# Output projection of a hybrid encoder layer: two blocks by seven products of quarters in place of eight

## The chip, the cores and the metric

The kernel runs on one core of one Trainium2 chip. The metric is the device time of one execution in microseconds (us); lower is better. A core has a matrix engine (TensorE, PE in the profile, with its weight loads as PEld), a vector engine (VectorE, DVE), a scalar engine (ScalarE, ACT), a general engine (GpSimd, POOL) and a queue that issues the transfers here (SyncE, SP). Each works through its own list of instructions in order and waits on semaphores for the others.

## The reference

One layer over 4096 tokens of width 1024, all float32:

```python
h = rmsnorm(x, pre_norm_g)
q, k, v, g_a, u_p, g_p = split(h @ w_in)            # 512, 128, 128, 512, 512, 512 columns
a = banded_attention(q, k, v, rel_bias, attn_sink) * silu(g_a)   # |i-j| <= 128, 8 query heads, 2 of k and v
p = multiscale_pool(u_p, pool_w, pool_scale) * silu(g_p)         # centred means over 2, 4, 8, 16 tokens
mixed = concatenate([a, p], -1) @ w_out             # (4096, 1024) @ (1024, 1024)
x = x + rmsnorm(mixed, post_norm_g)
```

The change touches the line of `mixed`, and what prepares its operands.

## The kernel before

Every float32 operand of a matmul is carried as a pair of float16 (high part and rest), so each product takes three matmuls: high·high, high·rest of the weights, rest·high.

**First phase** (from 0 to 541 us): eight tiles m of 512 tokens. For each, x is normalised, split into a pair (`x_split`, one `xp` tile per block of 128 tokens) and transposed by DMA into `xt`; then TensorE makes twelve projections of it: u, gp and ga, four each of 128 columns. ACT and DVE evacuate them; the pooled rows go to DRAM as float16 pairs (`yp_scr`), the gates as `ga_scr`, the x pairs as `x_scr`. The weights are scaled and split between, in a list `todo`; `prep_out`, which prepares w_out (8 tiles `wop`, 16 stores to `w_scr`), runs during tile 6. The `wop` tiles share the two buffers "xp" with the split x.

**Second phase** (from 541 us): pairs u of 128-token blocks, from u = 15 down, block 2u+1 ahead of 2u. TensorE's order is written by hand here (`manual_schedule`); the other engines' and SP's lists are ordered by the framework's scheduler. Per pair: `proj_kv`, two halves of `proj_q`; per block two halves of `softmax` (s on TensorE, the maximum on DVE, the exponential on ACT, the normalised pair `pn` on ACT and DVE, and a DMA transpose by SP to `pt`); `attend` (the attention output o on TensorE, gated on DVE, split on ACT and POOL into `ya`); `output` (96 matmuls of 512 columns per pair: for each block and each half of the columns 8 row blocks × 3, reading the pair `yb` of pooled rows from DRAM and `ya`), then squares on ACT, the norm's power on POOL, and the sum with x on DVE. `output` runs one block behind `attend`. The accumulators of kv, q and output rotate over three PSUM banks; there are two `pn` and four `pt` buffers.

Of the kernel before, what the change touches and what calls it, by code (L numbers as in the profile page):

```python
# [17 lines left out]
P = 128  # L18
# [8 lines left out]
PT_BUFS = 4  # L27
# [12 lines left out]
YLAG = 1  # L40

UT = 2 * P
NU = S // UT

# [8 lines left out]
GP_EVAC = 2.0**-29  # L53
GA_EVAC = 2.0**-43
# [4 lines left out]
def hybrid_layer(ctx: ExitStack, tc, io, out):  # L59
# [6 lines left out]
    gemm = ctx.enter_context(tc.tile_pool(name="gemm", bufs=3, space=PSUM))  # L66
# [27 lines left out]
    yp_scr = dram.tile([NB, P, 4, 2, P], F16, name="yp_scr")  # L94
    ga_scr = dram.tile([NB, P, 4, P], F32, name="ga_scr")
    w_scr = dram.tile([2, P, KT, D], F16, name="w_scr")
# [16 lines left out]
    def project(name, wh, wl, x, with_last=False):  # L113

        acc = gemm.tile([P, T], F32, name=name, tag="acc")
        a3 = acc.rearrange("p (b t) -> p b t", b=BPM)
        n = 0
        for k in range(KT):
            for w, kk in ((wh, k), (wl, k), (wh, KT + k)):
                mm = nc.tensor.matmul(  # L120
                    a3, w[:, k, :], x[:, :, kk, :], start=(n == 0), stop=(n == 3 * KT - 1)
                )
                n += 1
        return (acc, mm) if with_last else acc
# [5 lines left out]
    with ExitStack() as actx:  # L130
# [202 lines left out]
        def prep_out():  # L333
# [13 lines left out]
                out=rowsc[:, 0:4], in0=rowsc[:, 0:4], scalar1=2.0**23, scalar2=None, op0=ALU.mult  # L347
            )
            nc.vector.scalar_tensor_tensor(
                out=rowsc[:, 4:8], in0=rowsc[:, 4:8], scalar=2.0**24, in1=psc,  # L350
# [26 lines left out]
            for k in range(KT):  # L377
                w = pa.tile([P, D], F32, name=f"wo_b{k}", tag="wraw", bufs=4)
                nc.sync.dma_start(w, io["w_out"][k])
                s = rowsc[:, k : k + 1]  # L380
                wp = pa.tile([P, 2, D], F16, name=f"wop{k}", tag="xp", bufs=2)
                nc.scalar.activation(wp[:, 0], w, AF.Copy, scale=s)
                nc.vector.scalar_tensor_tensor(
                    out=wp[:, 1], in0=w, scalar=s, in1=wp[:, 0], op0=ALU.mult, op1=ALU.subtract
                )
                for i in range(2):
                    nc.sync.dma_start(w_scr[i, :, k, :], wp[:, i])
# [12 lines left out]
        def pool_tile(m, j, u, sg):  # L400

            yp = pa.tile([P, BPM, 2, P], F16, name=f"yp{m}_{j}", tag="yp")
            w = 2 << j
            cur, n = u, T + 16
            for lv in range(j + 1):
                n -= 1 << lv
                nxt = pa.tile([P, T + 16], F32, name=f"ws{m}_{j}_{lv}", tag="ws")
                nc.vector.tensor_tensor(
                    out=nxt[:, :n], in0=cur[:, :n], in1=cur[:, (1 << lv) : (1 << lv) + n],
                    op=ALU.add,  # L410
                )
# [16 lines left out]
            nc.gpsimd.tensor_tensor(out=t, in0=t, in1=sg, op=ALU.mult)  # L428
            t3 = t.rearrange("p (b t) -> p b t", b=BPM)
# [4 lines left out]
            nc.sync.dma_start(  # L434
                yp_scr[m * BPM : (m + 1) * BPM, :, j].rearrange("b p c d -> p b c d"), yp
            )
# [28 lines left out]
        first = gemm.tile([P, T], F32, name="gp0_0", tag="acc")  # L465
# [89 lines left out]
    wo_h = pb1.tile([P, KT, D], F16, name="wo_h")  # L555
    wo_l = pb1.tile([P, KT, D], F16, name="wo_l")
# [31 lines left out]
    def proj_kv(u):  # L588
        x = x_half(u)
        acc = gemm.tile([P, 2, UT], F32, name=f"kv{u}", tag="acc")  # L590
# [17 lines left out]
    def proj_q(u, half):  # L608

        x = x_half(u)  # L610
        if half == 0:
            q_t[u] = pb.tile([P, 2, 4, UT], F16, name=f"q{u}", tag="q")
        acc = gemm.tile([P, 2, UT], F32, name=f"q{u}_{half}", tag="acc")
        for jj in range(2):
            project_t(acc[:, jj], B_Q + 2 * half + jj, x)
        js = slice(2 * half, 2 * half + 2)
        split(q_t[u][:, 0, js], q_t[u][:, 1, js], acc)

    pt, y_t = {}, {}
# [4 lines left out]
    def softmax(b, half):  # L624
# [21 lines left out]
        for jj in range(2):  # L646
# [3 lines left out]
            for n, (qi, ki) in enumerate(((0, 0), (1, 0), (0, 1))):  # L650
                for c0, c1, kc in segs:
                    for gg in range(2):
                        a = slice(64 * gg, 64 * gg + 64)
                        nc.tensor.matmul(  # L654
                            s_ps[:, gg, c0:c1], q_t[u][a, qi, j0 + jj, tl : tl + P],
                            k_all[a, ki, kc : kc + c1 - c0], start=(n == 0 and c0 == 0),
                            stop=(n == 2 and c1 == nk), skip_group_check=True,
                        )
# [16 lines left out]
        pn = pb.tile([P, 2 * 4 * 3 * P], F16, name=f"pn{b}_{g}", tag="pn")  # L675
# [11 lines left out]
        nc.sync.dma_start(t4, pn[:, : 8 * nk], transpose=True)  # L687
        pt[b, half] = t4.rearrange("p (v g j k) q -> p v g j k q", v=2, g=2, j=2)

    def attend(b):  # L690
# [19 lines left out]
        y = pb.tile([P, 4, 2, P], F16, name=f"ya{b}", tag="ya", bufs=YLAG + 3)  # L710
        t = pb.tile([P, 4, P], F32, name=f"at{b}", tag="at")
        nc.vector.tensor_tensor(out=t, in0=o_ps, in1=ga, op=ALU.mult)  # L712
        nc.scalar.copy(y[:, :, 0], t)  # L713
        nc.gpsimd.tensor_tensor(out=y[:, :, 1], in0=t, in1=y[:, :, 0], op=ALU.subtract)  # L714
        y_t[b] = y

    def output(b):
        ya = y_t.pop(b)
        yp = pb.tile([P, 4, 2, P], F16, name=f"yb{b}", tag="yb")
        nc.sync.dma_start(yp, yp_scr[b])  # L720
        xr = pb.tile([P, D], F32, name=f"xr{b}", tag="xr")
        nc.sync.dma_start(xr, io["x"][b * P : (b + 1) * P, :])
        ss = pb.tile([P, 2], F32, name=f"ss{b}", tag="ss")
        mo = pb.tile([P, D], F32, name=f"mo{b}", tag="mo")
        for c in range(2):
            cs = slice(c * 512, (c + 1) * 512)
            acc = gemm.tile([P, 512], F32, name=f"mx{b}_{c}", tag="acc")
            n = 0
            for k in [4, 5, 6, 7, 0, 1, 2, 3]:
                y = yp[:, k - 4] if k >= 4 else ya[:, k]  # L730
                for yi, w in ((0, wo_h), (0, wo_l), (1, wo_h)):
                    nc.tensor.matmul(  # L732
                        acc, y[:, yi, :], w[:, k, cs], start=(n == 0), stop=(n == 3 * KT - 1)
                    )
                    n += 1
            junk = pb.tile([P, 512], BF16, name=f"jkb{b}_{c}", tag="junk", bufs=1)
            nc.scalar.activation(  # L737
                junk, acc, AF.Square, scale=2.0**-5, accum_out=ss[:, c : c + 1]
            )
            nc.vector.tensor_tensor(out=mo[:, cs], in0=acc, in1=gpost[:, cs], op=ALU.mult)  # L740
        ms = pb.tile([P, 1], F32, name=f"msb{b}", tag="ms")
        nc.vector.tensor_scalar(  # L742
            out=ms, in0=ss[:, 0:1], scalar1=ss[:, 1:2], scalar2=epss, op0=ALU.add, op1=ALU.add
# [3 lines left out]
        for cs in (slice(0, 512), slice(512, D)) if b == 0 else (slice(0, D),):  # L747
# [6 lines left out]

    with tc.manual_schedule(engines={mybir.EngineType.PE}):
# [3 lines left out]
        nc.sync.dma_start(wo_h, w_scr[0])  # L759
        nc.sync.dma_start(wo_l, w_scr[1])  # L760
# [3 lines left out]
        waiting = []  # L764
        for b in reversed(range(NB)):
            u = b // 2
            softmax(b, 0)
            if b == NB - 1:
                proj_q(u, 1)
                load_x(u - 2)  # L770
            if b % 2:
                if u > 0:
                    proj_kv(u - 1)
            else:
                if u > 0:
                    proj_q(u - 1, 0)
            if b == 0:
                output(waiting.pop(0))
            late = b in (NB - 2, NB // 2 - 1)
            if b + 1 < NB and not late:  # L780
                attend(b + 1)
                waiting.append(b + 1)
            softmax(b, 1)
            if b % 2 == 0 and u > 0:
                proj_q(u - 1, 1)
                load_x(u - 3)
            if late:
                attend(b + 1)
                waiting.append(b + 1)

            if len(waiting) > YLAG and b != NB // 2:
                output(waiting.pop(0))
        while waiting:
            output(waiting.pop(0))
        attend(0)
        output(0)
# [72 lines left out]
```

## Time and profile before

| | |
|---|---|
| median of 3 runs | 1282.33 us (1282.01 to 1283.87) |
| profiled execution | 1281.24 us, span 1279.4 us |
| first phase / second phase | 0 to 541 / 541 to 1279.4 us |
| matmuls of `mx` (output projection) | 1536, in four groups by operand of about 163, 163, 97 and 97 us busy |
| matmuls of all kinds | 8824 |

The profile shows one execution: busy time and count of each engine, groups of instructions by line with mean durations in ns, the chain of work that ended last, and the waits between engines. Matmuls overlap in the records, so what one costs is the distance from one to the next and not its duration. In a row such as `pt<-pn` the tile written stands left, the one read right. A row's bracket gives the engine's idle time ahead of it, and who ended it.

### The profile page before, as it was taken

What the parts mean: (1) busy time and instruction counts of PE and PEld (TensorE: products, weight loads), DVE (VectorE), ACT (ScalarE), POOL (GpSimd) and SP (SyncE); (2) the same over time, 40 slices, a digit from 0 to 9 for tenths busy, and PEclk for the clock granted to TensorE, in tenths of its full rate; (3) what the DMA queues carried; (4) which work ended last, traced back from release to release, by engine and by line L of the source; (5) the groups of instructions that cost most, each with busy time, mean ns of one, the idle gap of its engine ahead of it and who ended that gap; (6) DMA issues with size and microseconds to landing.
All of it is one profiled execution on the core that took longest, in us unless ns stands there. A gap on an engine that the chain in (4) does not pass through costs nothing. (4 is left out here: it accounts for less than half of the span.)

```text
span 1279.4 us, 22210 instructions
## 1 busy us (share of the span) xinstructions
PE 1245.6 (97%) x8824; PEld 718.4 (56%) x8824; DVE 732.0 (57%) x1609; ACT 588.4 (46%) x1271; POOL 197.5 (15%) x247
## 2 busy tenths in 40 slices
PE   4999999999999999999999999999999999999997
PEld 3643444444444444476666667577657666665643
DVE  5577373819151546456656557567656666575562
ACT  6365242515121541156555546456645555464451
POOL 1023131414030313301000101001100101010011
PEclk9998999999999999999999999999999999999999
DMA  7669385818170671287685777767666757755572
GB/s 229 231 162 288 145 217 146 256 49 277 52 206 25 204 224 42 70 264 169 169 186 132 174 165 160 162 158 172 167 161 154 191 138 171 178 143 128 126 191 90
DMA packets 331576, 210.19 MB, mean 164 GB/s; under 512 B 266656, under 2 KB 301088, under 8 KB 328528
## 3 DMA queue, kind: packets, MB, share of 16 engines
q1 hardware_dynamic: 331472, 208.78, 62.3%
q8 instruction: 69, 1.13, 0.4%
q14 instruction: 35, 0.29, 0.1%
HBM read 90.24 MB, written 52.99 MB: 112 GB/s over the span
## 5 line engine op out<-in xcount | busy, mean ns | idle before, releaser
L120 PEld LDWEIGHTS <-wa_h 128*128 128x128 f16 x1520 | 149.0, 98 | 184.9 <-issue 7.9
L667 ACT ACTIVATE p<-p,nm 128x385 f32<-128x385 f32 (+1 forms) x256 | 152.9, 599 | 49.3 <-POOL rsb L746 43.0
L583 PE MATMUL q<-xt,wb_h 128*128 128x256 f16 x1024 | 173.2, 273 | 0.0
L681 DVE SCALAR_TENSOR_TENSOR pn<-p,rd,pn 128x384 f16<-128x384 f32 (+1 forms) x256 | 139.4, 607 | 44.5 <-ACT pn L678 44.4
L732 PE MATMUL mx<-wo_h,ya 128*128 128x512 f16 x512 | 162.7, 379 | 0.2 <-POOL ya L714 0.2
L732 PE MATMUL mx<-wo_h,yb 128*128 128x512 f16 x512 | 162.9, 379 | 0.0
L120 PE MATMUL u<-xt,wa_h 128*128 128x512 f16 x512 | 155.7, 382 | 4.3 <-DVE xp L169 4.3
L662 DVE CUSTOM_DVE_ANT_0 p<-s,bias,nsink 128x384 f32<-128x384 f32 (+1 forms) x256 | 155.9, 664 | 0.5 <-PE s L654 0.5
L120 PE MATMUL ga<-xt,wa_h 128*128 128x512 f16 x512 | 153.6, 379 | 0.0
L678 ACT ACTIVATE pn<-p,rd 128x384 f16<-128x384 f32 (+1 forms) x256 | 134.6, 596 | 37.2 <-ACT p L667 36.7
L740 DVE TENSOR_TENSOR mo<-mx,gpost 128x512 f32<-128x512 f32 x64 | 44.1, 689 | 187.5 <-ACT jkb L737 187.3
L120 PE MATMUL gp<-xt,wa_h 128*128 128x512 f16 x496 | 149.0, 379 | 0.0
L583 PEld LDWEIGHTS <-wb_h 128*128 128x128 f16 x1280 | 125.2, 98 | 26.8 <-issue 12.7
L583 PE MATMUL q<-xt,wb_l 128*128 128x256 f16 x512 | 139.6, 273 | 0.0
L732 PEld LDWEIGHTS <-ya 128*128 128x128 f16 x768 | 75.1, 98 | 91.1 <-POOL ya L714 0.7
L737 ACT ACTIVATE jkb<-mx 128x512 bf16<-128x512 f32 x64 | 37.8, 591 | 192.0 <-PE mx L732 192.0
L120 PEld LDWEIGHTS <-wa_l 128*128 128x128 f16 x760 | 74.5, 98 | 88.6 <-issue 0.8
L732 PEld LDWEIGHTS <-yb 128*128 128x128 f16 x768 | 73.6, 98 | 88.6 <-issue 4.9
L120 PE MATMUL u<-xt,wa_l 128*128 128x512 f16 x256 | 98.0, 383 | 0.0
L120 PE MATMUL ga<-xt,wa_l 128*128 128x512 f16 x256 | 97.0, 379 | 0.0
L732 PE MATMUL mx<-wo_l,yb 128*128 128x512 f16 x256 | 97.0, 379 | 0.0
L732 PE MATMUL mx<-wo_l,ya 128*128 128x512 f16 x256 | 97.0, 379 | 0.0
(112 smaller groups left out, 1638.6 us busy)
## 6 DMA issues: line engine op xcount, KB each, us to landing
xn<-in_x SPq DMA_DIRECT2D x32, 512.0 KB, 5.7
xr<-in_x SPq DMA_DIRECT2D x32, 512.0 KB, 3.9
out<-xr SPq DMA_DIRECT2D x31, 512.0 KB, 2.7
x_scr<-xt SPq DMA_DIRECT2D x7, 2048.0 KB, 9.7
xt<-x_scr SPq DMA_DIRECT2D x14, 1024.0 KB, 6.0
ga_scr<-s_ga SPq DMA_DIRECT2D x32, 256.0 KB, 2.3
yp_scr<-yp SPq DMA_DIRECT2D x32, 256.0 KB, 2.4
gb<-ga_scr SPq DMA_DIRECT2D x32, 256.0 KB, 2.8
```

What stands on the lines that cost most here:

```text
L120: mm = nc.tensor.matmul(a3, w[:, k, :], x[:, :, kk, :], start=(n == 0), stop=(n == 3 * KT - 1))
L583: nc.tensor.matmul(a3, w[:, j, k, :], x[:, :, kk, :], start=(n == 0), stop=(n == 3 * KT - 1))
L662: nc.vector.tensor_tensor_reduce(out=p[:, hh, :nk], in0=s_t[jj][:, gg, :nk], in1=bias[:, h, lo : lo + nk], scale=negc[:, h : h + 1], scala ...
L667: nc.scalar.activation(p[:, hh, : nk + 1], p[:, hh, : nk + 1], AF.Exp, bias=nm[:, hh : hh + 1], scale=-1.0, accum_out=den[:, hh : hh + 1],)
L678: nc.scalar.activation(pn4[:, 0, hh], p[:, hh, :nk], AF.Copy, scale=rd[:, hh : hh + 1])
L681: nc.vector.scalar_tensor_tensor(out=pn4[:, 1, hh], in0=p[:, hh, :nk], scalar=rd[:, hh : hh + 1], in1=pn4[:, 0, hh], op0=ALU.mult, op1=ALU ...
L732: nc.tensor.matmul(acc, y[:, yi, :], w[:, k, cs], start=(n == 0), stop=(n == 3 * KT - 1))
L737: nc.scalar.activation(junk, acc, AF.Square, scale=2.0**-5, accum_out=ss[:, c : c + 1])
L740: nc.vector.tensor_tensor(out=mo[:, cs], in0=acc, in1=gpost[:, cs], op=ALU.mult)
```

## The change

The output of two blocks, [block 2u+1; block 2u], is a matrix of 2 × 2 quarters; the operand [a | p] has four quarters too (a11 and a21: attention rows of the odd and the even block; a12 and a22: their pooled rows), and w_out has four of 512 × 512. Strassen's scheme in Winograd's form makes the eight products of quarters from seven, with sums of quarters ahead (s1 to s4 of the rows; of the weights once, in the first phase) and behind (accumulators added on DVE). Each product is 12 matmuls of 512 columns, 84 per pair in place of 96. Products 2 and 3 accumulate into the bank of product 1 and of product 5. The row operands are `y11`, `y12`, `y22`, `ys1` to `ys4`; each is cast on ACT and its rest subtracted on POOL. The pooled rows stay float32 in DRAM and are split in the second phase. The weights are seven tiles `wo` of 1 MB, in place of two of 2 MB. Almost all tiles of the second phase have one buffer: `pn`, the halves of q, the seven `y`, `yf`, `mo`, and `pt` has three.

Core of the diff:

```diff
-PT_BUFS = 4
+PT_BUFS = 3
+PN_BUFS = 1
...
-    yp_scr = dram.tile([NB, P, 4, 2, P], F16, name="yp_scr")
+    yp_scr = dram.tile([NB, P, 4, P], F32, name="yp_scr")
...
-            for k in range(KT):
...
-                wp = pa.tile([P, 2, D], F16, name=f"wop{k}", tag="xp", bufs=2)
-                nc.scalar.activation(wp[:, 0], w, AF.Copy, scale=s)
...
-                for i in range(2):
-                    nc.sync.dma_start(w_scr[i, :, k, :], wp[:, i])
+            for k in range(HK):
+                ws = []
+                for kk in (k, HK + k):
...
+                for o, i0, i1 in (
+                    (ta[:, 0], w12, w11), (ta[:, 1], w22, ta[:, 0]),
+                    (tb[:, 0], w12, w22), (tb[:, 1], w21, ta[:, 1]),
+                ):
+                    nc.vector.tensor_tensor(out=o, in0=i0, in1=i1, op=ALU.subtract)
+                for o, n, f in (
+                    (O11, 1, w11), (O21, 2, ws[1]), (OT1, 2, ta.rearrange("p a c -> p (a c)")),
+                    (OT3, 2, tb.rearrange("p a c -> p (a c)")),
+                ):
+                    wp = pa.tile([P, 2, D], F16, name=f"wop{k}_{o}", tag="xp", bufs=2)
+                    nc.scalar.copy(wp[:, 0, : n * 512], f)
+                    nc.vector.tensor_tensor(
+                        out=wp[:, 1, : n * 512], in0=f, in1=wp[:, 0, : n * 512], op=ALU.subtract
+                    )
+                    for i in range(n):
+                        nc.sync.dma_start(
+                            w_scr[o + i, :, :, k, :], wp[:, :, i * 512 : i * 512 + 512]
+                        )
...
-            nc.scalar.copy(yp[:, :, 0, :], t3)
-            nc.gpsimd.tensor_tensor(
-                out=yp[:, :, 1, :], in0=t3, in1=yp[:, :, 0, :], op=ALU.subtract
-            )
...
-        pn = pb.tile([P, 2 * 4 * 3 * P], F16, name=f"pn{b}_{g}", tag="pn")
+        pn = pb.tile([P, 2 * 4 * 3 * P], F16, name=f"pn{b}_{g}", tag="pn", bufs=PN_BUFS)
...
+    def pair(u, name, f):
+        y = pb.tile([P, 4, 2, P], F16, name=f"y{name}_{u}", tag=f"y{name}", bufs=1)
+        nc.scalar.copy(y[:, :, 0], f)
+        nc.gpsimd.tensor_tensor(out=y[:, :, 1], in0=f, in1=y[:, :, 0], op=ALU.subtract)
+    def pool_in(u):
+        for i, name in ((1, "12"), (0, "22")):
+            f = pb.tile([P, 4, P], F32, name=f"yf{name}_{u}", tag=f"yf{name}", bufs=1)
+            nc.sync.dma_start(f, yp_scr[2 * u + i])
+    def operands_odd(u):
+        pair(u, "11", at[2 * u + 1])
+        pair(u, "22", yf[u, "22"])
+        pair(u, "12", yf[u, "12"])
+    def operands_even(u):
...
+        nc.vector.tensor_tensor(out=s1, in0=a21, in1=a22, op=ALU.add)
+        nc.vector.tensor_tensor(out=a21, in0=a21, in1=a11, op=ALU.subtract)
+        nc.vector.tensor_tensor(out=a11, in0=s1, in1=a11, op=ALU.subtract)
+        pair(u, "s2", a11)
+        pair(u, "s3", a21)
+        pair(u, "s1", s1)
+        nc.gpsimd.tensor_tensor(out=a12, in0=a12, in1=a11, op=ALU.subtract)
+        pair(u, "s4", a12)
+    def mix_p1(u):
+        x = acc_tile(u, "m1", 0)
+        product(x, u, "11", O11)
+        nc.scalar.copy(mo_t[u][0][:, HI], x)
+    def mix_p2(u, x):
+        product(x, u, "12", O21, add=True)
+        square(u, 0, 0, x)
+        nc.vector.tensor_tensor(out=mo_t[u][0][:, LO], in0=x, in1=gpost[:, LO], op=ALU.mult)
+    def mix_p5(u):
+        y = z_t[u] = acc_tile(u, "m5", 1)
+        product(y, u, "s1", OT1)
+        add(m1[:, HI], m1[:, HI], y)
+        square(u, 1, 1, m1[:, HI])
+        nc.gpsimd.tensor_tensor(out=m1, in0=m1, in1=gpost, op=ALU.mult)
+        finish(u, 1)
...
             if b % 2:
+                if u + 2 < NU:
+                    mix_p3(u + 2)
                 if u > 0:
                     proj_kv(u - 1)
+                pool_in(u)
+                if u + 1 < NU:
+                    attend(b + 1)
+                    operands_even(u + 1)
+                turned = softmax(b, 1)
...
+                if u + 1 < NU:
+                    x = mix_p1(u + 1)
+                    mix_p4(u + 1)
+                    mix_p2(u + 1, x)
+                    mix_p6(u + 1)
             else:
+                proj_q(u - 1, 0)
+                if b < NB - 2:
+                    attend(b + 1)
+                    operands_odd(u)
+                softmax(b, 1)
                 proj_q(u - 1, 1)
                 load_x(u - 3)
...
+                if u + 1 < NU:
+                    mix_p7(u + 1)
+                    mix_p5(u + 1)
```

How instructions stand on their engines, before and after, at three places.

ACT at the end of tile 6 in the first phase, before (`wop`: a weight tile of w_out; `xp`: a split block of tile 7; `s_ga`: a gate of tile 6):

```order
L382 ACTIVATE wop_3488<-wo_b_3486,rowsc 128x1024 [waits DMAHW5_49,DMAHW6_49,DMAHW1_49,DVE_49]
L394 ACTIVATE s_gp_3_3797<-gp_3_3772,cg 128x512 [waits PE_49]
L168 ACTIVATE xp_3673<-xn_3657,rs_3670 128x1024 [waits DMAHW7_49,DMAHW0_49,DVE_49]
L168 ACTIVATE xp_3684<-xn_3659,rs_3682 128x1024 [waits DMAHW2_49,DMAHW1_49,DVE_49]
L394 ACTIVATE s_ga_0_3847<-ga_0_3822,cg 128x512 [waits PE_49]
L168 ACTIVATE xp_3807<-xn_3661,rs_3805 128x1024 [waits DMAHW3_49,Pool_49]
L168 ACTIVATE xp_3818<-xn_3663,rs_3816 128x1024 [waits DMAHW4_49,Pool_49]
```

and after:

```order
L410 CAST wop_3_3491<-wo_t_3476 128x1024 [waits DMAHW2_49,DVE_49]
L410 CAST wop_5_3496<-wo_u_3477 128x1024 [waits DMAHW4_49,DMAHW3_49,DVE_49]
L424 ACTIVATE s_ga_3_3930<-ga_3_3905,cg 128x512 [waits DMAHW1_49,PE_49]
L180 ACTIVATE xp_3669<-xn_3653,rs_3666 128x1024 [waits DMAHW7_49,DMAHW6_49,DVE_49]
L180 ACTIVATE xp_3680<-xn_3655,rs_3678 128x1024 [waits DMAHW1_49,DMAHW0_49,DVE_49]
L180 ACTIVATE xp_3803<-xn_3657,rs_3801 128x1024 [waits DMAHW3_49,Pool_49]
L180 ACTIVATE xp_3814<-xn_3659,rs_3812 128x1024 [waits DMAHW4_49,Pool_49]
L533 ACTIVATE u_0_3934<-u_0_3935 128x512 [waits PE_49]
```

All four splits of tile 7 moved behind the last weight tile and behind the gate that evacuates tile 6's last projection.

ACT in the second phase between the second softmax half of the odd block and the first half of the even one, before (pair of blocks 23 and 22; `jkb`: the squares):

```order
L678 ACTIVATE pn_1_6903<-p_1_6865,rd_1_6864 128x384 [waits Activation_49]
L737 ACTIVATE jkb_0_6945,ss_6918<-mx_0_6920 128x512 [waits PE_49]
L737 ACTIVATE jkb_1_6973,ss_6918<-mx_1_6948 128x512 [waits PE_49,Activation_49]
L667 ACTIVATE p_0_6985,den_0_6983<-p_0_6985,nm_0_6982 128x385 [waits DVE_49,Pool_49]
L667 ACTIVATE p_0_6985,den_0_6983<-p_0_6985,nm_0_6982 128x385 [waits DVE_49] x3
L678 ACTIVATE pn_0_7011<-p_0_6985,rd_0_6984 128x384 [waits DMAHW6_49,DVE_49,Activation_49]
```

and after (`ys`: the operand s4 of pair 12; `y_11`: y22 and y12 of pair 11, from the rows `yf`):

```order
L700 ACTIVATE pn_1_6957<-p_1_6919,rd_1_6918 128x384 [waits Activation_49]
L744 CAST ys_12_6913<-yf_12_6238 128x4x128 [waits Pool_49]
L744 CAST y_11_7163<-yf_11_6856 128x4x128 [waits DMAHW7_49,PE_49]
L791 ACTIVATE jkb_00_7010,ss_6970<-m_12_6971 128x512 [waits PE_49]
L744 CAST y_11_7166<-yf_11_6854 128x4x128 [waits DMAHW3_49]
L689 ACTIVATE p_0_7030,den_0_7028<-p_0_7030,nm_0_7027 128x385 [waits DVE_49] x4
L700 ACTIVATE pn_0_7056<-p_0_7030,rd_0_7029 128x384 [waits DMAHW2_49,DVE_49,Activation_49]
```

Ahead of the four exponentials there now stand three casts, of which the last waits for a load.

SP in a pair, before (`yb`: pooled rows; `gb`: gates; `xr`: x for the sum):

```order
L687 DMA_TRANSPOSE pt_1_8288<-pn_1_8279 128x24x128 [waits DMAHW1_49,DVE_49]
L720 DMA yb_9158<-yp_scr 128x1024 [waits DMAHW2_49,PE_49]
L751 DMA out<-xr_8344 128x1024 [waits DMAHW3_49,DVE_49]
L722 DMA xr_9160<-in_x 128x1024 [waits DMAHW3_49]
L687 DMA_TRANSPOSE pt_0_8448<-pn_0_8439 128x24x128 [waits DMAHW5_49,DVE_49]
```

and after:

```order
L709 DMA_TRANSPOSE pt_0_6750<-pn_0_6741 128x24x128 [waits DMAHW6_49,DVE_49]
L751 DMA yf_11_6856<-yp_scr 128x512 [waits DMAHW7_49,DVE_49,Pool_49]
L855 DMA xr_7360<-in_x 128x1024 [waits DMAHW5_49,DMAHW0_49]
L717 DMA gb_7450<-ga_scr 128x512 [waits DMAHW1_49]
L709 DMA_TRANSPOSE pt_1_6966<-pn_1_6957 128x24x128 [waits DMAHW2_49,DVE_49,PE_49]
L751 DMA yf_11_6854<-yp_scr 128x512 [waits Pool_49]
L709 DMA_TRANSPOSE pt_0_7065<-pn_0_7056 128x24x128 [waits DMAHW4_49,DVE_49,PE_49]
```

The pooled rows used to be loaded some blocks ahead of their use, into one of two buffers; now each load waits for POOL's last reading of its only buffer, and the row of y12 (`yf_11_6854`) stands between two transposes.

More of the change, by code (lines that the diff above doesn't have):

```diff
@@ L709, in attend @@
                     n += 1
-        y = pb.tile([P, 4, 2, P], F16, name=f"ya{b}", tag="ya", bufs=YLAG + 3)
         t = pb.tile([P, 4, P], F32, name=f"at{b}", tag="at")
         nc.vector.tensor_tensor(out=t, in0=o_ps, in1=ga, op=ALU.mult)
[L713 to L720, printed above, removed]
+        at[b] = t
@@ new lines, in product, with load_wo @@
+    def product(acc, u, name, o, add=False):
+        y = y_t.pop((u, name))
+        n = 0
+        for k in range(HK):
+            for yi, wi in ((0, 0), (0, 1), (1, 0)):
+                nc.tensor.matmul(
+                    acc, y[:, k, yi, :], wo[o][:, wi, k, :], start=(n == 0 and not add),
+                    stop=(n == 3 * HK - 1), skip_group_check=True,
+                )
+                n += 1
+    def load_wo(o):
+        nc.sync.dma_start(wo[o], w_scr[o])
+    LO, HI = slice(0, 512), slice(512, D)
@@ new lines, in square, with acc_tile, add, mix_p4 @@
+    def square(u, i, c, src):
+        junk = pb.tile([P, 512], BF16, name=f"jkb{u}_{i}{c}", tag="junk", bufs=1)
+        nc.scalar.activation(
+            junk, src, AF.Square, scale=2.0**-5, accum_out=ss_t[u][:, 2 * i + c : 2 * i + c + 1]
+        )
+    def acc_tile(u, name, i):
+        return gemm.tile([P, 512], F32, name=f"{name}_{u}", tag=f"acc{i}")
+    def add(dst, a, acc):
+        nc.vector.tensor_tensor(out=dst, in0=acc, in1=a, op=ALU.add)
+    def mix_p4(u):
+        z_t[u] = acc_tile(u, "m4", 2)
+        product(z_t[u], u, "22", OT4)
@@ L724, in output @@
[L724 to L740, printed above, removed]
```

153 lines of the change are left out of this document (99 added, 54 removed).

## The prediction

> **What bounds the kernel now.** The page's first lines come first, then a stretch of 100 us in the second phase (its columns: TensorE, weight loads, DVE, ACT, POOL, granted clock, DMA), then the chain that ended last, inside it and at the end.
>
> ```profile
> span 1279.4 us, 22210 instructions
> PE 1245.6 (97%) x8824; PEld 718.4 (56%) x8824; DVE 732.0 (57%) x1609; ACT 588.4 (46%) x1271; POOL 197.5 (15%) x247
> 700.00:800.00 100.00, 100.00 (x905) 67.25 (x904) 63.84 (x159) 55.19 (x141) 9.71 (x18) 1.00 0.74 168
> 938.26 2.73 PE kv L583 x24
> ...
> 943.66 2.08 PE o L705 x36
> ...
> 972.24 10.36 PE mx L732 x48
> 982.60 1.08 PE s L654 x12
> 983.68 2.73 PE kv L583 x24
> ...
> 1264.70 7.53 PE mx L732 x34
> ```
>
> TensorE works 97% of the span; from 700 to 800 it never stops, and the chain there holds nothing but its matmuls. A pair of blocks takes 983.68 − 938.26 = 45.42 us. The output projection's matmul comes every 10.36/48 = 0.2158 us. The other engines have room on average, but what follows asks in which order their queues give it out.
>
> **1. Twelve matmuls a pair fewer.** 84 for 96, 16 pairs, all on the bound: 192 × 0.2158 = −41.4 us. TensorE's own work in a pair becomes 45.42 − 2.59 = 42.8 us: k and v 943.66 − 938.26 = 5.4, four score halves of 1.08, two attention products of 2.08, seven products of 2.59, and q with the 10.8 that are left.
>
> **2. The first phase.** Its 32 casts and 32 subtractions taken away were off TensorE, which waits for none of them: 0. The rows that are stored are as many bytes (float32 for two float16): 0. What counts is the place of the last token tile's split.
>
> ```profile
> 461.30 2.42 ACT L168 ACTIVATE xp<-xn,rs 128x1024 f16<-128x1024 f32 x2 [1.68 <-DMA w_scr<-wop]
> 470.24 3.67 SPq L172 DMA_TRANSPOSE xt<-xp  x2
> xt<-xp SPq DMA_TRANSPOSE x32, 4.1
> 478.86 0.38 PE L120 MATMUL u<-xt,wa_h 128*128 128x512 f16 x1
> 479.06 0.69 ACT L394 ACTIVATE s_ga<-ga,cg 128x512 f32<-128x512 f32 x1 [4.49 <-PE ga L120]
> ```
>
> Before, the four splits of tile 7 start at 461.30, the last transposes land near 472.1 + 4.1 = 476, and u's first matmul runs at 478.86 without a wait. After, the same four stand on ACT behind all sixteen weight tiles and behind the last evacuation of tile 6, the row at 479.06, so they start at 479.75 at the earliest. First split to last landing took 14.7 us: 494.5, a wait of 15.6. ACT can be later than that, since a weight tile can't be written before its two predecessors' stores (28 of them for 16) have landed; following the queue I get 24 to 26. I take 20; ends 10 (the stretch without the evacuations between) and 27.
>
> **3. A pair in the second phase: who is late.** TensorE's program order needs products one after another whose inputs come by ACT, DVE, POOL and SP; I followed those four queues in their new order, from the end of product 5's matmuls (time 0) to the next one. The rows:
>
> ```profile
> 948.17 0.62 ACT L667 ACTIVATE p<-p,nm 128x385 f32<-128x385 f32 x1
> 951.18 2.13 ACT L678 ACTIVATE pn<-p,rd 128x384 f16<-128x384 f32 x4 [0.50 <-ACT p L667]
> 954.06 3.67 SPq L687 DMA_TRANSPOSE pt<-pn  x1
> 953.69 0.19 ACT L737 ACTIVATION_READ_ACCUMULATOR jkb<-mx 128x1 f32 x1
> pt<-pn SPq DMA_TRANSPOSE x1, 5.5
> pt<-pn SPq DMA_TRANSPOSE x64, 6.5
> yb<-yp_scr SPq DMA_DIRECT2D x32, 256.0 KB, 2.9
> L662 DVE CUSTOM_DVE_ANT_0 p<-s,bias,nsink 128x384 f32<-128x384 f32 x240 | 148.2, 672 | 0.0
> L740 DVE TENSOR_TENSOR mo<-mx,gpost 128x512 f32<-128x512 f32 x64 | 44.1, 689 | 187.5 <-ACT jkb L737 187.3
> L748 DVE SCALAR_TENSOR_TENSOR xr<-mo,rsb,xr 128x1024 f32<-128x1024 f32 x31 | 39.7, 1280 | 1.6 <-POOL rsb L746 1.5
> L737 ACT ACTIVATE jkb<-mx 128x512 bf16<-128x512 f32 x64 | 37.8, 591 | 192.0 <-PE mx L732 192.0
> L713 ACT CAST ya<-at 128x512 f16<-128x512 f32 x32 | 19.8, 618 | 42.7 <-DVE at L712 42.7
> L714 POOL TENSOR_TENSOR ya<-at,ya 128x512 f16<-128x512 f32 x32 | 37.7, 1177 | 64.8 <-ACT ya L713 64.8
> L746 POOL TENSOR_TENSOR rsb<-msb,mhalf 128x1 f32<-128x1 f32 x32 | 17.5, 548 | 246.8 <-DVE msb L742 246.8
> 313.94 1.26 POOL L428 TENSOR_TENSOR yt<-yt,s_gp 128x512 f32<-128x512 f32 x1
> 314.09 1.69 DVE L408 TENSOR_TENSOR ws<-u 128x527 f32<-128x527 f32 x1
> 315.81 0.71 DVE L408 TENSOR_TENSOR ws<-ws 128x525 f32<-128x525 f32 x1
> 1262.34 1.28 DVE L748 SCALAR_TENSOR_TENSOR xr<-mo,rsb,xr 128x1024 f32<-128x1024 f32 x1
> 1262.94 1.70 POOL L714 TENSOR_TENSOR ya<-at,ya 128x512 f16<-128x512 f32 x1 [0.64 <-ACT ya L713]
> ```
>
> A softmax half is four exps, then the normalised halves pn (from 951.18 to 954.06, 2.9), then a transpose that SP issues: it holds SP 3.67, and lands 5.5 after its issue with nothing else under way (one seen alone), 6.5 by the median. With a single pn buffer the next pn waits for that landing.
>
> - First half, odd block. After product 5: sum 0.69, square 0.59 + 0.19, POOL's product with the post-norm over 1024 columns 2 × 1.26 = 2.5, pow 0.55, xr 1.28 on DVE, with den, rd and pn queued behind xr. Then product 3's sum, square, POOL 1.26, pow, and another xr between two of the four pn. Transpose issued at 12.9.
> - Second half. Evacuations of k and v (two half-width passes, some 1.3 in all) to 14.2, the attention output, then s1 and, between the four maxima, the two subtractions. These read two SBUF operands beside POOL: the rows at 1262.94 and 314.09 took 1.70 for 1.18, and 1.69 where the next took 0.71, each beside the other engine. I add 0.8 and 0.9. Last exp at 20.9, and the copy that product 1 leaves its bank by stands behind it on ACT: product 2, due at 1.08 + 2.59 + 5.40 + 2.08 + 1.08 + 2 × 2.59 = 17.4 by TensorE's own work, **waits 3.4**. pn from 21.6, with two of POOL's subtractions beside it; transpose issued at 26.7.
> - First half, even block. The load of the pooled row for y12 waits for POOL's last use of its only buffer, and stands on SP behind that transpose: 26.7 + 3.7 + 2.9 = 33.3. ACT has the cast of that row ahead of this half's exps. From there 0.62 + (954.06 − 948.17) = 6.5: transpose issued at 39.8, landed at 45.4.
> - Second half. Its pn waits for that landing, 2.9 to 48.3; behind it on ACT and DVE stands the evacuation of q's second half, 0.7, whose bank product 5 takes over: start at 49.0, end 51.6. TensorE would be there at 42.8 − 2.6 + 3.4 = 43.6: **5.4 waited** beside the 3.4, together 8.8.
>
> So the period is 51.6 against 42.8: 8.8 us a pair. The chain never passes through TensorE but at product 5, so TensorE's shorter work doesn't shorten it. Thirteen periods lie between the product 5 of the first pair and that of the third-last: 13 × 8.8 = +114. Its ends: 3.7 and 11.3 a pair, from the rivals below. What this adds to POOL (7 subtractions of 1.18, three products, 2 pow and one subtraction, about 14.2 us a pair) fits its idle time; only its places count.
>
> **4. Start and end of the second phase.**
>
> ```profile
> 541.02 0.27 PE L583 MATMUL kv<-xt,wb_h 128*128 128x256 f16 x1
> 560.33 6.79 SPq L687 DMA_TRANSPOSE pt<-pn  x1
> xt<-x_scr SPq DMA_DIRECT2D x14, 1024.0 KB, 6.0
> ```
>
> The first transpose is issued 19.3 us after the phase's first matmul. Before the first product 5, six more follow one by one, each after a landing (5.5 to 6.5) and a pn (2.9), then a pn, q's evacuation and the product (6.2): 19.3 + 7 × 5.5 + 6 × 2.9 + 6.2 = 81 at least, 88 by the median, and up to 104 with the waits of part 3 and five MB of weights loaded ahead of two of them (1 MB took 6.0). TensorE's own work to there is three pairs of kv and q, eight score halves, three attention products and six products: 48.6 + 8.6 + 6.2 + 15.5 = 79. +2 to +25; I take +18, since both kinds of wait are there. The end: four halves at part 3's spacing, then the last block's attention, sums, casts and five products, which nothing overlaps: about 74 from the last steady product 5, against 48.5 of own work and the 7.2 that lie before behind the last matmul (1264.70 + 7.53 = 1272.2, span 1279.4) with some 4 for the longer sums. +5 to +20, I take +14.
>
> **Sum.** The profiled execution took 1281.2 (1.1 below the runs' median). 1281.2 − 41.4 + 20 + 114 + 18 + 14 = 1405.8; I forecast 1406.
>
> **A rule of the skill against this.**
>
> ```profile
> 98.00:100.00 2.00, 1.22 (x3) 0.43 (x4) 0.73 (x2) 1.22 (x2) 0.00 (x0) 0.50 0.96 234
> 98.78 0.59 PE L120 MATMUL u<-xt,wa_h 128*128 128x512 f16 x1 [4.32 <-DVE xp L169]
> 99.17 0.63 PE L120 MATMUL u<-xt,wa_l 128*128 128x512 f16 x1
> ...
> 100.44 0.63 PE L120 MATMUL u<-xt,wa_l 128*128 128x512 f16 x1
> ```
>
> TensorE waited 4.32 us before 98.78, and the granted clock of the next 2 us was 0.50; the three matmuls from 99.17 to 100.44 came 0.42 apart instead of 0.216. The Trainium skill, "TensorE: Matmul & The Clock Gate", section "HAM oscillation — how this bites in real kernels", has the rule: leave TensorE no gap over about 3.4 us. The trace agrees with its one gap of 4.32. By it my 5.4 would halve the clock in every pair, and the forecast would be the first rival's.
>
> **Rivals.**
> - *The clock falls in each pair.* For it: the row at 98.78. Against: one such gap, and mine is an estimate that 1 us less brings below it. Product 5 then takes 12 × (0.42 − 0.216) = 2.5 us longer, and it is on the loop: 54.1 a pair, 13 × 2.5 = +33: 1439.
> - *Milder.* POOL and DVE don't meet (−1.7), and y12's row is loaded before the transpose that holds SP (−3.4). For it: the maxima, which take the longer part of that stretch, read only one operand from SBUF. Against: the queue's order has the transpose first. A period of 46.5, 13 × 3.7 = 48, start 10, end 8: 1281.2 − 41.4 + 20 + 66 = 1326.
> - *Faster: TensorE stays the bound.* If the scheduler's queues leave slack that I counted as waits, only step 2 is paid: 1281.2 − 41.4 + 18 = 1258. It decides where a pair's waits fall below (41.4 − 18)/16 = 1.5 us. For it: DVE 64%, ACT 55% busy in 700:800. Against: those shares hold no order, and four transposes with their pn in series take 4 × (5.5 + 2.9) = 33.6 of 42.8 without one wait.
>
> **How the numbers follow.** Main 0.45, clock 0.30, milder 0.15, faster 0.07, no change 0.03 (a balance near 1.5 a pair; ±0.2% is about what this measurement tells from none). The range runs from 1305, milder with part 2 at 10, the start at 2 and the end at 5 (1326 − 10 − 8 − 3), to 1453, the clock's case with part 2 at 27 and the start at 25 (1439 + 7 + 7). Faster and no change lie outside, with little of the others. Faster 0.07, same 0.03, slower 0.90.
>
> **What would show it.** TensorE's rows waiting for DVE ahead of product 5 (about 5 us) and for ACT ahead of product 2 (about 3); u of tile 7 waiting for its transpose some 20 us; kv rows 51 to 54 apart; pn on ACT waiting for a transpose's DMA. It would be wrong if the transposes in after land sooner, the pooled row's load isn't behind one, or TensorE stays above 95% busy.

## The result, and the profile after

The changed kernel takes 1416.78 us (median of 4 runs, 1415.42 to 1418.93), the kernel before 1283.1: 1.104 times as long, 95% interval 1.102 to 1.106. The forecast was 1406, the range 1305 to 1453. The profiled execution took 1417.87, its span 1416.1.

The page's first lines, and TensorE's longest waits (total in us, times, longest):

```profile
span 1416.1 us, 22192 instructions
PE 1247.9 (88%) x8632; PEld 709.7 (50%) x8632; DVE 837.6 (59%) x1714; ACT 639.2 (45%) x1351; POOL 336.8 (24%) x343
PE m L778 <- DVE q L597: 64.0, 14, 5.4
PE m L778 <- ACT mo L810: 26.8, 15, 2.3
PE u L132 <- DMA xt<-xp: 23.8, 1, 23.8
PE o L728 <- DMA pt<-pn: 9.4, 2, 6.3
```

TensorE has 192 matmuls fewer, and is busy 2 us longer: 88% of a longer span. Its waits stand where the prediction looked for them: ahead of product 5, until DVE has evacuated q (64.0); ahead of product 2, until ACT has copied product 1 out of its bank (26.8); and once for tile 7's transposes (23.8). The busy time did not fall by 41 because part of the work ran at half clock: by the granted clock over the whole trace this made TensorE's busy time 41 us longer (2 before), 23 of them in the thirteen pairs. The windows below show one place.

The start of tile 7: ACT's split x, SP's transposes, TensorE's first matmul.

```profile
486.03 1.15 ACT L180 ACTIVATE xp<-xn,rs 128x1024 f16<-128x1024 f32 x1 [0.78 <-DVE wop L411]
488.56 10.89 SPq L184 DMA_TRANSPOSE xt<-xp  x4
501.67 0.58 PE L132 MATMUL u<-xt,wa_h 128*128 128x512 f16 x1 [23.84 <-DMA xt<-xp]
```

Before, the split began at 461.30 and u at 478.86; now at 486.03 and 501.67.

One pair, from the timeline, between the product 5 that starts at 1020.46 and the next at 1072.32 (of each engine, the rows that carry it; the last row shows the 9 of 12 matmuls that begin before 1076):

```profile
1020.46 5.28 PE L778 MATMUL m<-wo,ys 128*128 128x512 f16 x12 [5.22 <-DVE q L597]
1037.63 4.42 SPq L709 DMA_TRANSPOSE pt<-pn  x1
1045.03 2.75 PE L778 MATMUL m<-wo,y 128*128 128x512 f16 x12 [1.40 <-ACT mo L810]
1050.28 3.68 SPq L709 DMA_TRANSPOSE pt<-pn  x1
1054.01 0.57 SPq L751 DMA_DIRECT2D yf<-yp_scr  x1
1056.79 0.62 ACT L744 CAST y<-yf 128x512 f16<-128x512 f32 x1 [7.49 <-DMA yf<-yp_scr]
1063.23 3.66 SPq L709 DMA_TRANSPOSE pt<-pn  x1
1068.81 2.13 ACT L700 ACTIVATE pn<-p,rd 128x384 f16<-128x384 f32 x4 [1.24 <-DMA pt<-pn]
1072.32 4.00 PE L778 MATMUL m<-wo,ys 128*128 128x512 f16 x9 [4.42 <-DVE q L597]
```

This is the prediction's walk, in its order of steps. The pooled row's load (1054.01) goes out only when the transpose at 1050.28 releases SP; ACT waits 7.49 us for it with the exponentials queued behind; the even block's transposes come late with it, q's evacuation stands behind the last pn, and product 5 waits. From 712.59 to 1330.81 there are twelve such periods: 51.52 us each.

The granted clock while product 5 runs (the third number from the end; TensorE's busy time stands behind the window's length):

```profile
1020.00:1022.00 2.00, 1.54 (x4) 0.56 (x4) 1.69 (x3) 0.24 (x1) 0.13 (x1) 0.50 0.52 102
1022.00:1024.00 2.00, 2.00 (x6) 0.76 (x5) 0.00 (x0) 0.48 (x2) 0.00 (x0) 0.50 1.14 217
```

Product 5 takes 5.2 us from its start to the next matmul's in this pair, 4.4 in the mean of the 13, and 2.7 in the first pair, where its wait was 0.5: 1.7 us a pair.

Where the 136.7 us of span went, by the first matmul of k and v, by the end of the first pair's product 5 and by that of the third-last:

| stage | forecast | measured |
|---|---|---|
| 192 matmuls fewer | −41.4 | −41.4 in the count; −39.1 alone (first experiment) |
| first phase | +20 | 566.75 − 541.02 = +25.7 |
| start of the second | +18 (97 for 79) | 665.2 − 566.75 = 98.4: +19 |
| 13 pairs | +114 (51.6 for 42.8) | 1334.9 − 665.2 = 669.7, 51.5 each: +113 |
| end | +14 (74 for 60) | 1416.1 − 1334.9 = 81.2: +21 |

### The profile page after: what moved, and what is told of

It is laid out like the page before. It is cut to its first block, busy times and chain, and to the rows that moved or that the text cites. A ratio compares the mean times of both kernels' runs of the same rounds, so it can differ in the third digit from the quotient of the medians.

```text
span 1416.1 us, 22192 instructions
## 1 busy us (share of the span) xinstructions
PE 1247.9 (88%) x8632; PEld 709.7 (50%) x8632; DVE 837.6 (59%) x1714; ACT 639.2 (45%) x1351; POOL 336.8 (24%) x343
## 4 chain that ended last, share of the span: by engine, by line
PE 24%; DVE 15%; DMA 8%; ACT 5%; POOL 4%; issue 2%; ACTq 0%; DVEq 0%; POOLq 0%; SPq 0%
PE m L778 11%; PE aq L607 9%; DMA pt<-pn 8%; DVE pn L703 5%; DVE xr L864 3%; POOL mo L838 2%; PE s L676 2%; PE o L728 2%; ACT pn L700 2%; DVE mo L799 1%; DVE p L684 1%; ACT p L689 1%; DVE at L765 1%; ACT jkb L791 1%; DVE s L763 1%
## 5 line engine op out<-in xcount | busy, mean ns | idle before, releaser
L778 PE MATMUL m<-wo,ys 128*128 128x512 f16 x768 | 202.4, 420 | 71.9 <-DVE q L597 64.0
L703 DVE SCALAR_TENSOR_TENSOR pn<-p,rd,pn 128x384 f16<-128x384 f32 (+1 forms) x256 | 174.8, 738 | 63.0 <-ACT pn L700 63.0
L132 PE MATMUL u<-xt,wa_h 128*128 128x512 f16 x512 | 157.3, 386 | 28.2 <-DMA xt<-xp 23.8
L607 PE MATMUL aq<-xt,wb_h 128*128 128x256 f16 x1024 | 173.2, 273 | 0.0
L778 PEld LDWEIGHTS <-ys 128*128 128x128 f16 x768 | 79.5, 105 | 183.1 <-issue 108.0
L778 PE MATMUL m<-wo,y 128*128 128x512 f16 x576 | 134.7, 389 | 30.0 <-ACT mo L810 26.8
L700 ACT ACTIVATE pn<-p,rd 128x384 f16<-128x384 f32 (+1 forms) x256 | 134.5, 596 | 41.8 <-DMA pt<-pn 34.4
L607 PE MATMUL aq<-xt,wb_l 128*128 128x256 f16 x512 | 139.6, 273 | 0.0
L778 PEld LDWEIGHTS <-y 128*128 128x128 f16 x576 | 55.7, 99 | 104.8 <-issue 41.1
L132 PE MATMUL gp<-xt,wa_l 128*128 128x512 f16 x248 | 94.0, 379 | 0.0
L457 POOL TENSOR_TENSOR yt<-yt,s_gp 128x512 f32<-128x512 f32 x32 | 45.4, 1418 | 197.6 <-DVE yt L453 124.0
L799 DVE TENSOR_TENSOR mo<-m,mo 128x512 f32<-128x512 f32 x80 | 54.8, 686 | 59.6 <-PE m L778 59.0
```

What stands on the lines that cost most here:

```text
L132: mm = nc.tensor.matmul(a3, w[:, k, :], x[:, :, kk, :], start=(n == 0), stop=(n == 3 * KT - 1))
L607: nc.tensor.matmul(a3, w[:, j, k, :], x[:, :, kk, :], start=(n == 0), stop=(n == 3 * KT - 1))
L700: nc.scalar.activation(pn4[:, 0, hh], p[:, hh, :nk], AF.Copy, scale=rd[:, hh : hh + 1])
L703: nc.vector.scalar_tensor_tensor(out=pn4[:, 1, hh], in0=p[:, hh, :nk], scalar=rd[:, hh : hh + 1], in1=pn4[:, 0, hh], op0=ALU.mult, op1=ALU ...
L778: nc.tensor.matmul(acc, y[:, k, yi, :], wo[o][:, wi, k, :], start=(n == 0 and not add), stop=(n == 3 * HK - 1), skip_group_check=True,)
L799: nc.vector.tensor_tensor(out=dst, in0=acc, in1=a, op=ALU.add)
```

## The experiments

Theory: the matmuls saved are saved, but TensorE is no longer the bound. A chain through ACT, DVE, POOL, SP and the transposes sets the pair's period; its longest single stop is the pooled row's load behind a transpose, and the half clock behind TensorE's wait adds to it. Rivals: the short buffers as such; POOL's hold on DVE; a clock that costs nothing because product 5 isn't on the loop. The kernel before took 1281.7 to 1281.9 beside these runs. A gain below is against the new kernel's 1416.8.

**The matmuls alone** (kernel before).

```diff
-            for k in [4, 5, 6, 7, 0, 1, 2, 3]:
+            for k in [4, 5, 6, 7, 0, 1, 2]:
```

> The kernel before with 84 instead of 96 output matmuls a pair and nothing else: one of the eight row blocks (k = 3) is left out of the product. If TensorE bounds the kernel before, as the first term of the sum says, the time falls by 192 x 0.2158 = 41 us, to about 1242. The rival, that another queue stands close behind TensorE, gives less than 30.

1242.74, ratio 0.969 (0.968 to 0.971): 39 us less. The first term holds: TensorE bounds the kernel before, and nothing stands close behind.

**The short buffers alone** (kernel before).

```diff
-PT_BUFS = 4
+PT_BUFS = 3
-        pn = pb.tile([P, 2 * 4 * 3 * P], F16, name=f"pn{b}_{g}", tag="pn")
+        pn = pb.tile([P, 2 * 4 * 3 * P], F16, name=f"pn{b}_{g}", tag="pn", bufs=1)
```

> The kernel before with the short buffers alone: one pn instead of two, three pt instead of four. Theory: what makes the new kernel late is the order of work ahead of each pn, not the buffers; four halves of 2.9 + 6.5 = 37.6 us fit into a pair's 45.4, so 0 to +10 us. Rival, the buffers cause most of the wait ahead of product 5: +60 us or more (4 to 5 us in each of 14 pairs).

1289.06, ratio 1.005 (1.004 to 1.007): +7, of which 4.7 are waits for transposes at the start (6.9 in place of 2.2). These two buffers alone, in the old order, are not the cause; the single buffers of `y`, `mo` and q were not tried by themselves.

**The first phase.** Buffers of their own for `wop` (room: one buffer less for a small tile).

```diff
-                    wp = pa.tile([P, 2, D], F16, name=f"wop{k}_{o}", tag="xp", bufs=2)
+                    wp = pa.tile([P, 2, D], F16, name=f"wop{k}_{o}", tag="wop", bufs=2)
```

> The new kernel with buffers of their own for the weight tiles wop, so that the last tile's split x is no longer behind them on ACT. Theory: the wait of 23.8 us at the start of tile 7 goes, with some 2 us of half clock behind it: 1417 - 24 to 26 = about 1392. Rival, the weight tiles' stores and loads make the transposes late whatever the order: less than 10 us.

1394.18: −22.6. The wait of 23.8 is gone from TensorE's list (0.5 is left at that place, at 484.19). On ACT tile 7's last split now starts at 450.37 and the last weight tile is cast at 495.56, behind it: shared buffers had set the order.

**The clock.**

```diff
+        y3 = y_t[u, "s3"]
+        product(x, u, "s3", OT3)
+        y_t[u, "s3"] = y3
         product(x, u, "s3", OT3)
```

> The new kernel with product 7 issued twice into the same bank (12 matmuls a pair more, the second time over the first), which fills half of TensorE's wait ahead of product 5. Clock theory: the wait falls from about 5 to 2.4 us, the clock stays at 1.0, product 5 takes 2.7 instead of 4.4 us and is on the loop: 13 x 1.7 = -22 us, to about 1395, although TensorE has 192 matmuls more. Rival, product 5 is slow for another reason or is not on the loop: 0; and if TensorE were the bound, +41.

1411.97: −4.8, not −22. Two of its product 5, with a short and with a long wait ahead:

```profile
863.15 2.75 PE L778 MATMUL m<-wo,ys 128*128 128x512 f16 x12 [1.84 <-DVE q L597]
1013.76 4.44 PE L778 MATMUL m<-wo,ys 128*128 128x512 f16 x12 [4.32 <-DVE q L597]
```

Where the wait fell to about 1.9 (nine of thirteen pairs), product 5 took 2.7 and the period was 49.4: 2.1 less than 51.5, though TensorE had 2.6 more to do. So the clock is a cause, and product 5 is on the loop. In the other four the wait stayed at 2.5 to 4.3 (ahead of the first, second and fourth of them the odd block's second transpose landed 7.1, 7.1 and 6.2 us after its issue, where 5.5 is the median; why is open), and the clock fell again. The mean period is 50.55, so 12 to 13 us were won in the loop; the second product 7 costs 5 at the end, where nothing hides it, and the first phase's wait was 1.6 longer. My price left the end out.

**The pooled row's load, twice.** First a second buffer for the row of y12 (one for the gates in exchange):

```diff
-            f = pb.tile([P, 4, P], F32, name=f"yf{name}_{u}", tag=f"yf{name}", bufs=1)
+            f = pb.tile([P, 4, P], F32, name=f"yf{name}_{u}", tag=f"yf{name}", bufs=2 if name == "12" else 1)
-        ga = pb.tile([P, 4, P], F32, name=f"gb{b}", tag="gb")
+        ga = pb.tile([P, 4, P], F32, name=f"gb{b}", tag="gb", bufs=1)
```

> The new kernel with two buffers for the pooled row of y12, so that its load no longer stands behind the odd block's second transpose (the gates gb get one buffer instead of two to make room). Theory: the cast of that row holds up the even block's first half; without it that half's pn starts with the landing of the transpose before, 30 us after product 5 instead of 34.5, the wait ahead of product 5 falls below 1 us, the clock stays up, and the period is 44.7 to 46: 13 x 5.5 to 6.8 = -72 to -88, to 1329 to 1345. Rival, the single pn buffer binds: less than 15 us, since the pn would wait for the landing at once.

Then without a buffer more:

```diff
-        nc.gpsimd.tensor_tensor(out=a12, in0=a12, in1=a11, op=ALU.subtract)
-        pair(u, "s4", a12)
+        nc.gpsimd.tensor_tensor(out=a21, in0=a12, in1=a11, op=ALU.subtract)
+        pair(u, "s4", a21)
```

> The new kernel with one line changed: POOL writes the difference y12 - s2 for s4 into the tile of s3's rows instead of over the pooled row. The row's buffer then comes free before the odd block's second transpose and the scheduler puts its load ahead of that transpose; no buffer is added. Theory (the late load of that row, not its buffer as such, holds the loop): the same gain as with two buffers, about 1360. Rival, the gain of the two buffers came from something else in that kernel: above 1400.

1360.5 and 1360.17: −56 and −57, from two different edits that have only the early load in common. SP's rows in the second kernel, and ACT's waits in the new kernel and in this one:

```profile
1016.52 0.32 SPq L751 DMA_DIRECT2D yf<-yp_scr  x1
1020.37 12.13 SPq L709 DMA_TRANSPOSE pt<-pn  x2
```

```profile
ACT y L744 <- DMA yf<-yp_scr: 105.0, 15, 8.4
ACT pn L700 <- DMA pt<-pn: 34.4, 20, 4.8
```

```profile
ACT pn L700 <- DMA pt<-pn: 77.3, 33, 4.8
```

The load is ahead of the two transposes; ACT's 7 us a pair for the row are gone from its longest waits, and part of them has turned into waits of pn for its one buffer (34.4 to 77.3). The transposes landed after 6.2 us in the median, too, in place of 5.5. Both fit a period that fell to 46.9 and 47.1 and not to 44.7; the expectation was some 15 us too low.

**Two pn buffers alone** (room: one gates buffer less, three `v` for four, s1 over y22's row).

```diff
-PN_BUFS = 1
+PN_BUFS = 2
```

> The new kernel with two pn buffers (room: one gates buffer less, three v instead of four, s1 written over the row of y22). Theory: in the pair at 1020 us the pn of the even block's second half starts 0.9 us after its exponentials, by the landing; the rest of the wait is older: 13 x 0.9 = -12, to about 1405. Rival, the single buffer makes the chain: -50 or more.

1398.94: −18. The period fell by 0.66 to 50.86, and the waits for transposes at the start from 9.4 to 4.1. With the row's load still behind the transpose, the second buffer is worth little.

**POOL's readings.** Zeros in place of the seven rests, in the new kernel and in the one with the difference elsewhere:

```diff
-        nc.gpsimd.tensor_tensor(out=y[:, :, 1], in0=f, in1=y[:, :, 0], op=ALU.subtract)
+        nc.gpsimd.memset(y[:, :, 1], 0.0)
```

> The new kernel where POOL writes zeros in place of the rests of the seven row operands and so reads nothing there (the rests are left out of the product). Theory, DVE's two-operand passes are held up while POOL reads: the two subtractions of quarters go from 1.3 to 0.7 us and four pn from 4.0 to 2.2, 3.0 us a pair on the loop, with part of the clock loss: 13 x 3 to 4 = -40 to -52, to 1365 to 1377. Rival, those rows are long for themselves and not by POOL: 0 to -5.

> The one-line kernel (difference elsewhere) where POOL again writes zeros in place of the seven rests and reads nothing there. The row's load is ahead in both kernels now, so the difference is what POOL's readings cost DVE: 1.2 us in the two subtractions ahead of product 2 and 1.8 in pn. Theory: 2 to 3 us a pair until TensorE binds, 1360 - 26 to 39 = 1321 to 1334. Rival, the whole gain of the zeros came by the earlier load: 0 to -8.

1345.59 (−71) and 1345.04 (−15 against 1360.2). The first is confounded: zeros wait for no cast, so the pooled row's buffer came free early and its load went ahead of the transpose. In the second comparison both kernels have the load ahead. DVE's groups with POOL reading, in the kernel with the difference elsewhere (xcount | busy us, mean ns):

```profile
L703 DVE SCALAR_TENSOR_TENSOR pn<-p,rd,pn 128x384 f16<-128x384 f32 x236 | 164.7, 753 | 92.7 <-ACT pn L700 92.7
...
L765 DVE TENSOR_TENSOR at<-at,at 128x512 f32<-128x512 f32 x15 | 18.6, 1238 | 0.0
L766 DVE TENSOR_TENSOR at<-s,at 128x512 f32<-128x512 f32 x15 | 18.4, 1229 | 0.0
```

and without:

```profile
L703 DVE SCALAR_TENSOR_TENSOR pn<-p,rd,pn 128x384 f16<-128x384 f32 x240 | 142.2, 648 | 83.3 <-ACT pn L700 83.3
...
L765 DVE TENSOR_TENSOR at<-at,at 128x512 f32<-128x512 f32 x15 | 10.3, 686 | 0.0
L766 DVE TENSOR_TENSOR at<-s,at 128x512 f32<-128x512 f32 x15 | 10.3, 685 | 0.0
```

The rows are longer by POOL's reading and not by themselves: 1.24 against 0.69, and 0.75 against 0.65 for each of sixteen pn, 2.8 us of DVE a pair. The period fell by only 1.2 (47.1 to 45.9). That is not what POOL's readings cost the loop, since the zeros bring a wait of their own. In each of 13 pairs one small row of DVE (`den`, 128x4), which took 0.17 us, now takes 1.72, beside POOL's subtraction for s4 and the zeroing behind it, and ACT's pn waits for it:

```profile
735.94 1.72 DVE L693 TENSOR_SCALAR den<-den 128x4 f32<-128x4 f32 x1 [0.17 <-ACT p L689]
737.95 2.13 ACT L700 ACTIVATE pn<-p,rd 128x384 f16<-128x384 f32 x4 [1.06 <-issue]
```

So this pn starts 20.2 us after product 5, where it started at 19.9 with the longer subtractions: their 1.1 us never reached it. Zeros also take POOL 0.52 us a row in place of 1.2 to 1.4. The 1.2 is a balance of all this; what POOL's readings alone cost the loop, and whether the 2 to 3 expected was right, stays open.

**Together.** Row ahead by a second buffer, and own `wop`:

> The new kernel with both changes, the row of y12 loaded ahead and own buffers for wop. Both theories give the sum of their gains: 1329 to 1345 less 23 (as measured) = 1306 to 1322, still slower than before (1282), since the start (+19), the end (+21) and some 2 us of waits at product 2 in each pair stay. Rival: the gains overlap, above 1330.

1339.96: the sum of the two gains as measured (−56 − 23 = −79, measured −77), so they do not overlap; the expectation was 18 too low, about as that of the row alone. Then the difference elsewhere, own `wop` and two pn:

> The line of the run before, own buffers for wop, and two pn (one gates buffer, three v, s1 over y22's row). With the row ahead, the pn of the even block's two halves waited 1.3 and 2.8 us for a landing; with two pn these go, until TensorE itself and its wait of 1.75 ahead of product 2 bind, 42.8 + 1.8 = 44.6 a pair: 1340 (row and wop) - 13 x 2.3 - 5 at the start = about 1305. Rival, something else in the chain stands close behind: 1325 or more.

1295.9, ratio 1.011 (1.009 to 1.013): −121, the best of the new scheme here, and still slower than before. Its waits and a stretch of 400 us, beside that stretch of the new kernel (the second row of windows):

```profile
PE m L778 <- ACT mo L810: 24.9, 14, 2.2
...
PE m L778 <- DVE q L597: 2.5, 1, 2.5
700.00:1100.00 400.00, 384.31 (x3475) 256.70 (x3474) 313.98 (x671) 245.40 (x611) 140.91 (x143) 1.00 0.70 165
```

```profile
700.00:1100.00 400.00, 347.43 (x2952) 222.81 (x2950) 274.10 (x588) 214.56 (x534) 122.15 (x124) 0.96 0.58 145
```

The wait ahead of product 5 is down to one, the clock is 1.00, and the period is 44.75: TensorE's 42.8 and the 1.75 that it waits for ACT's copy ahead of product 2. Two pn, worth 18 alone, are worth 44 here (1340 to 1296; the two ways of loading the row early had given the same time), 9 more than expected: they had become the next stop. What keeps it above 1282, against the sum −41: first phase +7 (548.05 for 541.02), start +14, 13 pairs × 1.95 = +25, end +13 (73.4 for 60).

**The scores ahead of product 2** (in the kernel of the run before).

```diff
-                    mix_p2(u + 1, x)
-                    mix_p6(u + 1)
+                    px[u + 1] = x
...
             turned = softmax(b, 0)
+            if b % 2 == 0 and u + 1 in px:
+                mix_p2(u + 1, px.pop(u + 1))
+                mix_p6(u + 1)
```

> As the run before, with the even block's first scores on TensorE ahead of product 2 instead of behind product 6, which puts 1.08 us of work into the wait ahead of product 2. If TensorE with that wait is the loop by now: 13 to 15 x 1.1 = -14 to -16 against the run before, about 1290. Rival, the loop is still the softmax chain: 0 to -5.

1361.82: 66 slower, where 14 to 16 faster was expected. TensorE's waits, and DVE's row that ends them:

```profile
PE aq L607 <- DVE mo L816: 56.8, 14, 4.3
...
PE m L778 <- ACT mo L810: 7.1, 13, 0.5
```

```profile
815.54 0.69 DVE L816 TENSOR_TENSOR mo<-m,gpost 128x512 f32<-128x512 f32 x1 [0.19 <-ACT jkb L791]
```

The wait ahead of product 2 did fall to 0.5. But with the scores earlier, their maxima and exponentials went ahead of product 2's square on ACT and its evacuation on DVE, and q's first half needs product 2's bank: 4.3 us of wait there at most, 4.1 in the mean, and the clock with it.

## Why the prediction was right

The sum came within 0.8% of the median, and each term but the end within 6 us of its stage.

- *Twelve matmuls fewer*: right, 39 alone against 41.4.
- *First phase, +20*: right in place and cause (own buffers take it away); the wait itself was 23.8 and the stage +25.7, nearer to the upper figure of the queue's walk (24 to 26) than to the 20 taken.
- *Pair, 51.6*: the period is right (51.5), its parts are not. In the pair shown, by times from product 5's end (1025.67), the first transpose was issued at 12.0 (forecast 12.9), the second at 24.6 (26.7), y12's cast ran at 31.1 (33.3), the third transpose was issued at 37.6 (39.8), and product 5 started at 46.7 (49.0). The walk was 2.3 too long by product 5, and 0.9 of that stood already at the first transpose. Against it product 5 ran at reduced clock: +1.7 a pair on average, up to +2.5. The main case assumed full clock and kept the fall as a rival at 0.30. So the number rests on two errors of opposite sign, a chain over-priced by about 2 and the clock left out; that they cancel is luck. The place of the waits, the order of causes and the load behind the transpose were right. The wait ahead of product 2 was 1.8 on average for a forecast of 3.4; the forecast ran to the last exponential (20.9) and left out the copy behind it (0.56), which would have made it longer still, but this moves time between TensorE's two waits and not the period.
- *The clock rival*: its mechanism occurred in all 13 pairs; its price (1439) was not reached because the chain was shorter and product 5 lost 1.7, not 2.5. The rule of the Trainium skill ("TensorE: Matmul & The Clock Gate", section "HAM oscillation — how this bites in real kernels") spoke rightly against the change: all waits here were 4.4 us or more. Its 3.4 us is no safe side, though; shorter waits cost too (last section).
- *The milder rival* named the right mechanism as the largest: with the load ahead the period falls by 4.4 to 4.6, more than the 3.4 it was priced at, as the clock recovers with it. POOL's part, priced at 1.7, showed as 1.2 net of a wait that the experiment itself brought, so its size is open.
- *Faster*: TensorE stays the bound only when the load, the buffers and the first phase are all mended, and even that kernel is 1% slower than before.
- *The end*: +21 for +14, the term that was sized worst. With nothing to overlap, TensorE waits six times in the last pair for a sum, a cast or a subtraction, among them 2.1, 1.1, 1.9 and 2.1 us for y and ys. The clock fell there too: half clock made TensorE's busy time 7.8 us longer in this stage, about the 7 that the term was short; no experiment set this apart.

## What to carry to other kernels

When TensorE bounds a kernel at 97%, work taken off it pays only as far as the next chain is shorter; add that chain up in each queue's own order before the change, since shares of 55 to 64% say nothing of it. A single-buffered tile whose reload is issued from a queue that also issues transposes makes the load wait for its last reader and for whatever is ahead of it in the queue; writing an intermediate elsewhere can free it without memory. And stops stand one behind the other: the second pn buffer was worth 18 us alone, 44 once the load was out of the way, and moving one group of matmuls into a gap cost 66 because its results went ahead of a bank's release.

## What the runs showed of the hardware

The clock falls after shorter gaps than expected. In eight profiles with product 5 behind a wait (the new kernel's and those of seven variants), its time to the next matmul was 2.7 in 55 of 56 cases with a wait under 2.1 us, 4.0 to 4.4 in 16 of 24 with 2.1 to 2.7, over 3.9 in 8 of 9 with 3 to 4, and 4.0 to 5.2 in all 21 above 4.

Which gaps cost follows from where they lie. In all 14 traces the granted clock changes only at steps of 3.41 us, on a grid that runs on through the whole trace. Counted from 20 us on, a step at full clock in which TensorE was busy for less than 1.36 us was followed by one at half clock in all 138 cases, one with more than 1.50 in none of 4993, and in between in 11 of 25. From half clock it came back after every step with at least 2.67 us busy (137) and after none with less (112). Two waits of the same length in the kernel with a second buffer for the row, 2.60 us ahead of 709.72 and 2.61 ahead of 1084.65 (length, TensorE busy, granted clock, DMA share, GB/s):

```profile
705.46:708.87 3.41, 1.65 (x8) 1.00 0.88 303
708.87:712.28 3.41, 2.56 (x12) 1.00 0.70 133
```

```profile
1080.92:1084.34 3.42, 1.12 (x6) 1.00 0.74 278
1084.34:1087.75 3.41, 3.10 (x8) 0.50 0.83 159
```

The first wait spans the border of two steps and leaves 1.65 us of work in the earlier one; the second lies almost whole in one step, leaves 1.12, and product 5 runs at half clock behind it (4.2 us for 2.7). So a gap of 2.1 to 2.7 us may or may not cost, and a gap above 4 always did here.

A transpose's landing isn't one number: its median was 5.5 us after its issue in the new kernel and 6.2 in the two with the row ahead, and single ones took 7.0 to 7.5. With the second buffer two in consecutive pairs (837.62 and 884.81) took 7.1 and 7.2, with a load issued 4.8 us before them; but in the kernel with the difference elsewhere two took 7.2 and 7.3 (885.34 and 1076.00) with no other transfer issued in the 9 us before. What makes the difference was not tried and stays open.
